# Splitting the last 512 tokens 384 + 128 instead of 256 + 256, and giving GpSimd two of the last eight multiplies

## The chip, the cores and the metric

The kernel runs on one core of a Trainium2 chip. The metric is the device time of one execution in microseconds (us). Three timed runs of the kernel before gave 1228.05, 1231.03 and 1229.72 us; their median is 1229.72 us.

The core has five engines that each work off their own queue in order: TensorE (PE in the profile; its weight loads are listed apart, as PEld), VectorE (DVE), ScalarE (ACT), GpSimd (POOL) and SyncE (SP), which here issues all DMA transfers. Engines wait for one another by semaphores. In this kernel TensorE writes its results to an accumulator memory, PSUM, from which VectorE and ScalarE read; everything else on the chip is held in the main memory of the engines, SBUF.

## What is computed

Two residual layers over 1024 tokens with 1024 features, each with a mixer (`h = RMSNorm(x) * (1 + scale(c)) + shift(c)`, then `x <- x + gate(c) * mixer(h)`), and a last RMSNorm. The change touches only the end: the output projection of the second mixer, its residual, and the last norm.

```python
    out = rms_norm(out, ...)                 # inside the mixers
    return (out * jax.nn.silu(g)) @ w_out    # odd mixer: the projection of the last stage
    ...
    x = x + gate[:, None, :] * y
return rms_norm(x, final_g)                  # x * rsqrt(mean(x*x) + eps) * final_g
```

## The kernel before

All data are held with the features on the 128 partitions and the tokens along the columns, so x is eight tiles ("slabs") of 128 features, each in two halves of 512 tokens (`HF`). A matrix product in float32 accuracy is made of three products of split operands (`mm3`, lines 196 to 199): high by high, high by low and low by high part. Each of the three loads a weight tile of 128 x 128 and then streams the tokens of the segment as its columns.

The last stage is lines 1259 to 1277, with `out_layer` (lines 939 to 1006). It goes through the tokens in three segments, `(0, 0, 0, 512)`, `(0, 1, 0, 256)` and `(0, 1, 256, 512)`: the first half of the tokens whole, then the second half in two pieces of 256. For every segment, `run` makes eight output slabs. One slab c is

- 8 x 3 products into one PSUM bank (`proj`, line 226; lines 197 to 199 in the profile, tile `pp`). There are four banks in turn;
- `evac`, line 960: VectorE adds the gated product to the residual x, in place (line 962, tile `xh`); ScalarE squares it (line 967, tile `sq`); VectorE adds the square to the sum of those before (line 973). In the last segment the square of the last slab isn't added but goes to TensorE by itself (lines 969 to 971), to spare a step at the end.

When a segment's eight slabs are done, `tail` (line 982) finishes the norm: TensorE sums the squares over the partitions with a tile of ones (`ss_add`, line 323, tile `ssl`), ScalarE takes the root (line 346, `rs`), VectorE the reciprocal (line 347, `rr`), TensorE spreads it over all partitions (`spread`, line 352, tile `bc`, in PSUM), and `finish` (line 1261) multiplies each slab by the norm's gain g and by `bc` (VectorE, line 1263) and stores it (SyncE, line 1265). Matrix products in full float32, such as those of lines 323 and 352, are two passes each in the profile: four calls are x8.

The loop at the end sets the order: with each slab of a segment, two steps of the tail of the segment before are issued (`some(before, 2)`), so the tails of the first two segments lie beside the products of the next. The tail of the last segment has nothing beside it. SyncE's queue takes the eight stores of a tail in the order of the slabs, 0 to 7. All weights of this stage are in SBUF, split into their two parts, by the end of its first segment: GpSimd's last work before the change (line 182) is there.

Of the kernel before, what the change touches and what calls it, by code (L numbers as in the profile page):

```python
# [11 lines left out]
F32 = mybir.dt.float32  # L12
F32R = mybir.dt.float32r
I32 = mybir.dt.int32
AF = mybir.ActivationFunctionType
ALU = mybir.AluOpType
# [3 lines left out]
P = 128  # L20
# [3 lines left out]
HF = 512  # L24
EPS = 1e-6
NEG = -1.0e38
LR = 12
SQ = 4
NM = (2, 2, 2)
NW = (3, 3, 3, 3)  # L30
# [18 lines left out]
O_FG = 72  # L49
# [47 lines left out]
def kernel(ctx, tc, xT, xTp, small, lamp, adaw, tb, w0, gw, wo0, w1, nab, wo1, out):  # L97
    nc = tc.nc
    V, A, G, T = nc.vector, nc.scalar, nc.gpsimd, nc.tensor
# [16 lines left out]
    sm = const.tile([P, N_SMALL], F32, tag="sm", name="sm")  # L116
# [93 lines left out]
    def wide(on):  # L210
        state["wide"] = on
# [3 lines left out]
    def split_act(k, hf, src, eng):  # L215
        hi = actp.tile([P, HF], F32R, tag=f"hi{k}_{hf}", name=f"ahi{k}_{hf}")
        lo = actp.tile([P, HF], F32R, tag=f"lo{k}_{hf}", name=f"alo{k}_{hf}")
        A.activation(hi[:], src, AF.Copy)
        eng.tensor_tensor(lo[:], src, hi[:], ALU.subtract)
        hact[k, hf] = (hi, lo)  # L220
# [5 lines left out]
    def proj(i, hf, evac, korder=range(KC), prep=True, view=lambda x: x, cols=(0, HF)):  # L226
        ks = list(korder)
        wh, wl = slab(i)
        ps = bank(f"pp{i}_{hf}")[:, :cols[1] - cols[0]]
        for n, k in enumerate(ks):  # L230
            hi, lo = (t[:, cols[0]:cols[1]] for t in hact[k, hf])
            mm3(ps, wh[:, k, :], wl[:, k, :], view(hi), view(lo), n == 0, n == KC - 1)
            if n % 2 == 1 and n < KC - 1:
                yield 1300.0
        with tc.high_priority():
            evac(hf, ps)
        if prep:
            ahead(i + 1)
        yield 1300.0
# [78 lines left out]
    def ss_start(name):  # L318
        return ptp.tile([P, HF], F32, tag="pt", name=name)

    def ss_add(ss, sq, start, stop, w=P):
        for j in range(4):
            T.matmul(ss[32 * j:32 * j + 32, :w], ones[:], sq[:, j * w:(j + 1) * w],
                     start=start, stop=stop)

    def rstd_rows(ss, n, pool, spare=None, add=EPS):


        if spare is not None:
            v, rr, t = (spare[:, i * P:(i + 1) * P] for i in range(3))  # L330
        else:
            v, rr, t = (pool.tile([P, P], F32, tag=g, name=g)[:] for g in ("rs", "rr", "rt"))
        V.tensor_scalar(v, ss[:, :P], 1.0 / n, add, ALU.mult, ALU.add)
        V.tensor_scalar(rr.bitcast(I32), v.bitcast(I32), -0.5, float(0x5F3759DF),
                        ALU.mult, ALU.add)
        for _ in range(3):
            V.scalar_tensor_tensor(t, rr, -0.5, rr, ALU.mult, ALU.mult)
            V.tensor_tensor(t, t, v, ALU.mult)
            V.scalar_tensor_tensor(rr, t, 1.5, rr, ALU.add, ALU.mult)
        return rr  # L340

    def rstd_rows_act(ss, n, pool, w):

        v = pool.tile([P, P], F32, tag="rs", name="rs")
        rr = pool.tile([P, P], F32, tag="rr", name="rr")
        A.activation(v[:, :w], ss[:, :w], AF.Sqrt, bias=eps[:], scale=1.0 / n)
        V.reciprocal(rr[:, :w], v[:, :w])
        return rr

    def spread(rr, bc, w=P):  # L350
        for j in range(4):
            T.matmul(bc[:, j * w:(j + 1) * w], sel[:, j, :], rr[:, :w], start=True, stop=True)
# [105 lines left out]
    with tc.tile_pool(name="start", bufs=2) as stp, tc.tile_pool(name="ada0", bufs=12) as adp:  # L458
# [11 lines left out]
        def squares(hf, on_dve, pool, tag):  # L470
# [4 lines left out]
            for k in range(KC):  # L475
                sq = stp.tile([P, HF], F32, tag="sq", name="sq", bufs=SQ)
                if k in on_dve:
# [5 lines left out]
        bcs = {}  # L483
# [131 lines left out]
    def some(gen, n):  # L615
        for _ in range(n):
            next(gen, None)
# [8 lines left out]
    with tc.tile_pool(name="lru", bufs=1) as lp:  # L626
# [34 lines left out]
        def pair(cs_):  # L661
# [3 lines left out]
            for c in cs_:  # L665
                xc, xh, xl = xcs[c]
                wh, wl = gws.pop(c)
                for r in range(2):
                    for g in range(2):
                        t = lp.tile([P, S], F32, tag="lr", name=f"t{g}", bufs=LR)  # L670
                        tt[c, r, g] = t
                        i = r * 2 + g
                        o = O_GB + (r * 2 + g) * 4 + c
                        for hf in range(2):
# [4 lines left out]
                            yield 648.0  # L679
                    w = ws[c, r] = lp.tile([P, S], F32, tag="lr", name="w", bufs=LR)  # L680
                    o = r * 4 + c
# [257 lines left out]
    def out_layer(l, ato, xsrc, xdst, pool, korder, view, segments):  # L939

        xs, acc, sums = {}, {}, {}

        def run(s):
            i0, hf, lo, hi = segments[s]
            n, w = hi - lo, (hi - lo) // 4

            def load(k):
                if k < KC and (k, hf) not in xs:  # L950
                    t = pool.tile([P, HF], F32, tag="xh", name=f"xh{l}_{hf}_{k}",
                                  bufs=11 if l == 0 else 16)
                    nc.sync.dma_start(t[:], xsrc[k * P:(k + 1) * P, hf * HF:(hf + 1) * HF])
                    xs[k, hf] = t

            load(0)
            for c in range(KC):
                load(c + 1)

                def evac(hf_, ps, c=c):  # L960
                    x = xs[c, hf][:, lo:hi]
                    state["dve"] = V.scalar_tensor_tensor(  # L962
                        x, ps, modc[l][:, 16 + c:17 + c], x, ALU.mult, ALU.add).ins
                    if xdst is not None:
                        nc.sync.dma_start(xdst[c * P:(c + 1) * P, hf * HF:(hf + 1) * HF], x)
                    sq = pool.tile([P, HF], F32, tag="sq", name="sq", bufs=3)
                    A.activation(sq[:, :n], x, AF.Square)
                    last = l and s == len(segments) - 1
                    if c == KC - 1 and last:
                        ss_add(sums[s], sq, False, True, w)  # L970
                        return
                    if c:
                        V.tensor_tensor(sq[:, :n], sq[:, :n], acc[s][:, :n], ALU.add)
                    acc[s] = sq
                    if c == KC - 2 and last:
                        sums[s] = ss_start(f"ssl{l}_{s}")
                        ss_add(sums[s], sq, True, False, w)
                for _ in proj(ato + i0 + c, hf, evac, korder, view=view, cols=(lo, hi)):
                    pass
                yield  # L980

        def tail(s, final):
            _, hf, lo, hi = segments[s]
            w = (hi - lo) // 4
            if s not in sums:
                sums[s] = ss_start(f"ssl{l}_{s}")
                with tc.issue_after(state["pe"]):
                    ss_add(sums[s], acc[s], True, True, w)
            if xdst is None:
                rr = rstd_rows_act(sums[s], D, pool, w)  # L990
            else:
                rr = rstd_rows(sums[s], D, pool)
                yield
            bc = ptp.tile([P, HF], F32, tag="pt", name=f"bc{l}_{s}")
            with tc.issue_after(state["pe"]):
                spread(rr, bc, w)
            yield
            for k in range(KC):
                final(k, hf, lo, xs[k, hf][:, lo:hi], bc[:, :hi - lo])
                yield  # L1000

        for hf in range(2):
            for k in korder:
                split_act(k, hf, mixed[k][:, hf * HF:(hf + 1) * HF],
                          G if l == 0 and k >= 4 else V)
        return run, tail
# [251 lines left out]

    wide(True)
    with tc.tile_pool(name="fin", bufs=2) as fp:  # L1260
        def finish(k, hf, lo, x, bc):
            g = sm[:, O_FG + k:O_FG + k + 1]
            V.scalar_tensor_tensor(x, x, g, bc, ALU.mult, ALU.mult)
            t0 = hf * HF + lo
            nc.sync.dma_start(out[k * P:(k + 1) * P, t0:t0 + x.shape[1]], x)


        segments = ((0, 0, 0, 512), (0, 1, 0, 256), (0, 1, 256, 512))
        run, tail = out_layer(1, ato1, x1d, None, fp, KORDER1, lambda x: x, segments)
        before = iter(())  # L1270
        for s in range(len(segments)):
            r = run(s)
            for c in range(KC):
                some(r, 1)
                some(before, 2)
            before = tail(s, finish)
        some(before, KC + 1)
# [100 lines left out]
```

## Time and profile before

| | |
|---|---|
| timed runs | 1228.05, 1229.72, 1231.03 us |
| profiled execution | 1229.11 us, its span 1227.2 us |
| PE, PEld busy in the span | 1177.9 us (96%), 969.2 us (79%) |
| DVE, ACT, POOL busy | 725.6 us (59%), 553.5 us (45%), 376.3 us (31%) |
| granted TensorE clock | 0.995 |

Times in the views are us from the start of the span; means of groups are in ns. `out<-in` names the tiles that an instruction writes and reads, and `128x256` is partitions by columns. A chain of waits follows the work that ended last back from step to step; "issue" in it is time in which the profile shows no wait. The ends of matrix products and weight loads are modelled by the profiler, so their starts say more than their durations.

### The profile page before, as it was taken

Reading aid. Unit: us, or ns where it says so; the run is one execution under the profiler, and the core shown is the slowest. Engines: PE = TensorE matmul, PEld = TensorE weight load, DVE = VectorE, ACT = ScalarE, POOL = GpSimd, SP = SyncE. Lnnn points to the kernel's source line nnn. Section 1 sums busy time; section 2 is a strip of 40 time slices with the busy share of each in tenths; the row PEclk is TensorE's granted clock in tenths of the full one; section 3 lists DMA queues with packets and bytes.
Section 4 is the critical chain, followed back from the end, with each engine's and each line's share of the span. In section 5 each row is a group of like instructions: output and inputs, shape, how many; then the busy total and the mean of one; then the engine's idle time right before and its main releaser. Section 6 shows DMA issues by size and latency. Waiting matters only on the chain.

```text
span 1227.2 us, 19073 instructions
## 1 busy us (share of the span) xinstructions
PE 1177.9 (96%) x7232; PEld 969.2 (79%) x7232; DVE 725.6 (59%) x1418; ACT 553.5 (45%) x1023; POOL 376.3 (31%) x348
## 2 busy tenths in 40 slices
PE   4989999799999999999999999999999999999997
PEld 3578887678888888777778888888988898877896
DVE  6762966899899889668672433453333323464344
ACT  3337658456666556423342333443344324375121
POOL 2113432133243334533422323333323333244100
PEclk9999999999999999999999999999999999999999
DMA  9610153232123110286424443333332333223312
GB/s 330 188 38 27 60 170 105 69 101 78 42 63 108 46 57 20 84 284 205 149 72 149 124 145 109 117 116 108 100 108 81 103 105 106 76 81 113 136 69 70
DMA packets 81467, 132.24 MB, mean 108 GB/s; under 512 B 7008, under 2 KB 48096, under 8 KB 81376
## 3 DMA queue, kind: packets, MB, share of 16 engines
q1 hardware_dynamic: 81376, 131.03, 34.1%
q8 instruction: 57, 0.93, 0.3%
q14 instruction: 34, 0.28, 0.1%
HBM read 110.03 MB, written 14.68 MB: 102 GB/s over the span
## 4 chain that ended last, share of the span: by engine, by line
PE 82%; DVE 10%; DMA 3%; ACT 2%; POOL 1%; issue 1%; SPq 0%; DVEq 0%; ACTq 0%; POOLq 0%
PE pp L197 16%; PE pp L199 16%; PE pp L198 15%; PE no L1226 4%; PE etr L1202 3%; PE v L197 3%; PE v L198 2%; PE v L199 2%; PE atr L857 2%; PE s L599 2%; PE s L600 2%; PE n L599 2%; PE n L600 2%; PE o L198 1%; PE o L197 1%
## 5 line engine op out<-in xcount | busy, mean ns | idle before, releaser
L197 PE MATMUL pp<-ahi,whi 128*128 128x512 f32 (+1 forms) x1040 | 405.9, 390 | 3.7 <-DVE sgb L605 3.3
L199 PE MATMUL pp<-ahi,wlo 128*128 128x512 f32 (+1 forms) x1040 | 397.4, 382 | 2.5 <-POOL wlo L182 2.5
L198 PE MATMUL pp<-alo,whi 128*128 128x512 f32 (+1 forms) x1040 | 395.8, 381 | 0.0
L182 POOL TENSOR_TENSOR wlo<-raw,whi 128x1024 fp32r<-128x1024 f32 x80 | 196.1, 2454 | 333.5 <-ACT whi L181 330.0
L197 PEld LDWEIGHTS pp<-ahi,whi 128*128 128x128 f32 x1040 | 196.3, 189 | 45.8 <-issue 9.6
L199 PEld LDWEIGHTS pp<-ahi,wlo 128*128 128x128 f32 x1040 | 196.3, 189 | 41.1 <-POOL wlo L182 3.4
L198 PEld LDWEIGHTS pp<-alo,whi 128*128 128x128 f32 x1040 | 196.5, 189 | 32.2 <-issue 0.7
L1182 DVE CUSTOM_DVE_ANT_0 e<-n,bias 128x288 f32<-128x288 f32 (+1 forms) x128 | 60.4, 504 | 151.8 <-PE n L600 76.7
L181 ACT ACTIVATE whi<-raw 128x1024 fp32r<-128x1024 f32 x80 | 84.3, 1055 | 133.4 <-PE pp L198 88.2
L1190 POOL TENSOR_SCALAR e<-e,r 128x288 f32<-128x288 f32 (+1 forms) x128 | 72.3, 577 | 180.0 <-DVE r L1188 178.0
L1185 ACT ACTIVATE e<-e,nm 128x288 f32<-128x288 f32 (+1 forms) x128 | 72.8, 570 | 111.9 <-DVE nm L1182 111.2
L831 ACT ACTIVATE e<-e,nm 128x1024 f32<-128x1024 f32 x64 | 73.4, 1148 | 38.3 <-DVE nm L827 37.7
L827 DVE CUSTOM_DVE_ANT_0 e<-s,tb 128x1024 f32<-128x1024 f32 x64 | 76.9, 1216 | 3.9 <-DMA tb<-in_tb_dram 2.6
L197 PE MATMUL v<-whi,ahi 128*128 128x256 f32 x256 | 74.7, 292 | 0.0
L198 PE MATMUL v<-wlo,ahi 128*128 128x256 f32 x256 | 72.5, 283 | 0.0
L199 PE MATMUL v<-whi,alo 128*128 128x256 f32 x256 | 72.3, 282 | 0.0
L848 POOL TENSOR_SCALAR e<-e,r 128x256 f32<-128x256 f32 x32 | 32.9, 1028 | 100.6 <-DVE r L837 42.4
L1226 PE MATMUL no<-et,vc 96*64 96x128 f32 (+1 forms) x768 | 60.6, 282 | 0.0
L1226 PEld LDWEIGHTS no<-et,vc 96*64 96x64 f32 (+1 forms) x768 | 42.2, 136 | 21.5 <-issue 19.3
L864 ACT ACTIVATE ath<-atr 128x512 fp32r<-128x512 f32 x64 | 38.0, 596 | 45.7 <-PE atr L857 45.4
L1206 ACT ACTIVATE et<-etr 96x384 f32<-96x384 f32 (+1 forms) x64 | 31.2, 487 | 58.8 <-DVE et L1208 53.7
L962 DVE SCALAR_TENSOR_TENSOR xh<-pp,mod,xh 128x512 f32<-128x512 f32 (+1 forms) x40 | 25.7, 643 | 53.8 <-PE pp L199 47.7
(206 smaller groups left out, 2007.6 us busy)
## 6 DMA issues: line engine op xcount, KB each, us to landing
raw<-in_w_dram SPq DMA_DIRECT2D x56, 512.0 KB
ada<-in_adaw_dram SPq DMA_DIRECT2D x96, 256.0 KB
raw<-in_wo_dram SPq DMA_DIRECT2D x24, 512.0 KB
bias<-in_nab_dram SPq DMA_DIRECT2D x32, 288.0 KB
qq<-qq SPq DMA_DIRECT2D x48, 128.0 KB
bias<-in_nab_dram SPq DMA_DIRECT2D x16, 384.0 KB
xT<-in_xT_dram SPq DMA_DIRECT2D x16, 256.0 KB
xh<-in_xTp_dram SPq DMA_DIRECT2D x16, 256.0 KB
```

The costliest lines, as they stand in the source:

```text
L181: A.activation(hi[:], raw[:], AF.Copy)
L182: G.tensor_tensor(lo[:], raw[:], hi[:], ALU.subtract)
L197: T.matmul(ps, lh, rh, start=start, stop=False)
L198: T.matmul(ps, lh, rl, start=False, stop=False)
L199: state["pe"] = T.matmul(ps, ll, rh, start=False, stop=stop).ins
L599: T.matmul(dst, qsel(q[m]), k, start=True, stop=False)
L827: state["dve"] = V.tensor_tensor_reduce(out=e[:], in0=ps[:].rearrange("p a b -> p (a b)"), in1=tbt[h][:, o:o + S], scale=-1.0, scalar=3.0e ...
L831: A.activation(e[:], e[:], AF.Exp, scale=-1.0, bias=nm[:], accum_out=sums[:, m:m + 1])
L1182: state["dve"] = V.tensor_tensor_reduce(out=e[:, m, :n], in0=ps[:, m, :n], in1=bias["now"][:, m, :n], scale=-1.0, scalar=3.0e38, op0=ALU.a ...
L1185: A.activation(e[:, m, :n], e[:, m, :n], AF.Exp, scale=-1.0, bias=nm[:, m:m + 1], accum_out=sums[:, m:m + 1])
L1190: state["pool"] = G.tensor_scalar(e[:, m, :n], e[:, m, :n], r[:, m:m + 1], 0.0, ALU.mult, ALU.add).ins
L1226: T.matmul(po[64 * m:64 * m + 64, b * P:(b + 1) * P], vch[p, b][:kn, j + hf, 64 * m:64 * m + 64], et[:kn, m, j * P:(j + 1) * P], start=(j ...
```

## The change

Two edits in the last stage.

First, the border between the last two segments moves from token 256 of the second half to token 384 (`LAST`): the middle segment has 384 tokens, the last 128.

Second, in the last segment slabs 0 and 1 (`EARLY`) are finished in another way. Right after their square is taken, ScalarE multiplies them by the gain g, in place. When `bc` is there, ScalarE copies it to an SBUF tile (`bcs`), and GpSimd multiplies the two slabs by that tile. The other six are multiplied by VectorE as before. The stores stay on SyncE, in the order 0 to 7.

```diff
+LAST = 384
+EARLY = (0, 1)
...
                     A.activation(sq[:, :n], x, AF.Square)
                     last = l and s == len(segments) - 1
+                    if last and c in EARLY:
+                        A.activation(x, x, AF.Copy, scale=sm[:, O_FG + c:O_FG + c + 1])
...
+        spread_ = {}
+
         def finish(k, hf, lo, x, bc):
             g = sm[:, O_FG + k:O_FG + k + 1]
-            V.scalar_tensor_tensor(x, x, g, bc, ALU.mult, ALU.mult)
+            if lo == LAST and k in EARLY:
+
+                if not spread_:
+                    spread_[0] = fp.tile([P, P], F32, tag="bcs", name="bcs", bufs=1)
+                    A.activation(spread_[0][:], bc, AF.Copy)
+                G.tensor_tensor(x, x, spread_[0][:], ALU.mult)
+            else:
+                V.scalar_tensor_tensor(x, x, g, bc, ALU.mult, ALU.mult)
...
-        segments = ((0, 0, 0, 512), (0, 1, 0, 256), (0, 1, 256, 512))
+        segments = ((0, 0, 0, HF), (0, 1, 0, LAST), (0, 1, LAST, HF))
```

## The prediction, made before the changed kernel was run

> **What bounds the kernel now.** I read the page first, for the span:
>
> ```profile
> span 1227.2 us, 19073 instructions
> ```
>
> The profiled execution took 1229.11 us, 1.91 us more than its span and 0.61 us less than the median of the three runs, 1229.72 us. The change touches only the last stage, so the next view is the busy time by stretches, for one inside the 512-token segment and one inside the last segment (256 tokens).
>
> ```profile
> 1145.00:1168.00 23.00, 23.00 (x105) 19.11 (x105) 6.94 (x10) 2.53 (x4) 0.32 (x1) 1.00 0.06 23
> 1198.00:1215.00 17.00, 17.00 (x144) 17.00 (x142) 7.94 (x19) 2.50 (x6) 0.00 (x0) 1.00 0.19 63
> ```
>
> The columns are the stretch's length, then PE, PEld, DVE, ACT and POOL busy, then the granted clock. TensorE (PE) has no idle time in either, so up to the last product the stage is bound by TensorE. The second number is the weight loads (PEld): 19.11 of 23.00 us with 512 columns to a product, but 17.00 of 17.00 with 256. With half the columns, a load is in flight at every moment.
>
> Then the chain that ended last, after TensorE's last product:
>
> ```profile
> 1217.03 0.49 DVE xh L962
> 1217.53 0.02 issue
> 1217.55 0.42 ACT sq L967
> 1217.97 0.04 issue
> 1218.02 0.36 PE ssl L323 x8
> 1218.38 0.02 issue
> 1218.40 0.32 ACT rs L346
> 1218.73 0.02 issue
> 1218.75 0.56 DVE rr L347
> 1219.31 0.14 issue
> 1219.45 1.09 PE bc L352 x8
> 1220.54 0.02 issue
> 1220.56 0.48 DVE xh L1263
> 1221.04 0.39 DVEq L1372
> 1221.44 2.35 DVE xh L1263 x6
> ```
>
> Here each step waits for the one before. From 1217.03 to the end of the span are 10.2 us, and only this tail can become shorter by a smaller last segment. Its last part isn't VectorE's but SyncE's:
>
> ```profile
> 1221.07 3.76 SPq L1265 DMA_DIRECT2D out_dram<-xh  x8
> ```
> ```profile
> L1265 SPq DMA_DIRECT2D out_dram<-xh x24: 332/361/403, 1175.7 to 1224.4; - x24
> ```
>
> VectorE is done at 1223.79 (1221.44 + 2.35), and SyncE's eighth issue ends at 1224.83. The second row gives the shortest, median and longest issue in ns. With 0.36 us for the last one, the starts are (3.76 − 0.36)/7 = 0.486 us apart, slower than the multiplies (2.35/6 = 0.39). The span ends 2.37 us after the last issue.
>
> **The change, part 1: what TensorE pays.** Each output slab has 8 × 3 = 24 products in every segment, whatever its number of tokens. The pitch of slabs is seen in the starts of VectorE's evacuations. With 512 columns, then with 256:
>
> ```profile
> 1151.38 0.75 DVE L962 SCALAR_TENSOR_TENSOR xh<-pp,mod,xh 128x512 f32<-128x512 f32 x1 [3.24 <-PE pp L199]
> 1152.83 0.69 DVE L973 TENSOR_TENSOR sq<-sq 128x512 f32<-128x512 f32 x1 [0.70 <-ACT sq L967]
> 1156.82 0.75 DVE L962 SCALAR_TENSOR_TENSOR xh<-pp,mod,xh 128x512 f32<-128x512 f32 x1 [3.30 <-PE pp L199]
> ```
> ```profile
> 1207.96 0.48 DVE L962 SCALAR_TENSOR_TENSOR xh<-pp,mod,xh 128x256 f32<-128x256 f32 x1 [1.42 <-PE pp L199]
> 1208.93 0.43 DVE L973 TENSOR_TENSOR sq<-sq 128x256 f32<-128x256 f32 x1 [0.48 <-ACT sq L967]
> 1210.84 0.48 DVE L962 SCALAR_TENSOR_TENSOR xh<-pp,mod,xh 128x256 f32<-128x256 f32 x1 [1.49 <-PE pp L199]
> ```
>
> 1156.82 − 1151.38 = 5.44 us per slab, 0.2267 per product; 1210.84 − 1207.96 = 2.88, 0.120 per product. So 256 columns cost 0.1067 us and each product 0.0133 besides. On that line 384 columns cost 4.16 us a slab (0.173 a product) and 128 cost 1.60 us (0.067). If the line held to the end, moving 128 tokens from one segment to the other would cost TensorE nothing: 4.16 + 1.60 = 2 × 2.88.
>
> I don't think that it holds below 256, because every product loads a weight tile of 128 columns, and the loads are already back to back. What such a load costs when little streams behind it is shown by the broadcast of line 352: eight passes, each with a 128-column weight load and only 64 columns.
>
> ```profile
> 1219.42 0.97 PEld L352 LDWEIGHTS bc<-rr,sel 128*128 128x128 f32 x8 [1.25 <-issue]
> ```
>
> The groups by form (the number after the bar's comma is the mean in ns) have the duration of one such load, and the pieces that the rest of the sum needs:
>
> ```profile
> L962 DVE SCALAR_TENSOR_TENSOR xh<-pp,mod,xh 128x256 f32<-128x256 f32 x16 | 7.7, 484 | 18.3 <-PE pp L199 18.3
> ...
> L1263 DVE SCALAR_TENSOR_TENSOR xh<-xh,sm,bc 128x512 f32<-128x512 f32 x8 | 5.7, 740 | 0.4 <-PE bc L352 0.4
> ...
> L352 PEld LDWEIGHTS bc<-rr,sel 128*128 128x128 f32 x24 | 2.9, 191 | 1.3 <-issue 1.2
> ...
> L962 DVE SCALAR_TENSOR_TENSOR xh<-pp,mod,xh 128x512 f32<-128x512 f32 x2 | 1.5, 752 | 6.6 <-PE pp L199 6.6
> ...
> L967 ACT ACTIVATE sq<-xh 128x512 f32<-128x512 f32 x2 | 1.3, 632 | 9.6 <-DVE xh L962 9.6
> ...
> L323 PE MATMUL ssl<-sq,ones 128*32 128x64 f32 x24 | 1.0, 231 | 1.0 <-ACT sq L967 1.0
> L347 DVE RECIPROCAL rr<-rs 128x128 f32<-128x128 f32 x1 | 1.0, 952 | 0.3 <-ACT rs L346 0.3
> ...
> L323 PE MATMUL ssl<-sq,ones 128*32 128x128 f32 x8 | 0.4, 285 | 0.0
> ```
>
> With 0.19 us for the last of the eight loads, their starts are (0.97 − 0.19)/7 = 0.111 us apart. How long 64 columns stream in these full-precision passes is seen in line 323: 64 more of them cost 285 − 231 = 54 ns. By the slab pitch 128 columns of this stage's products cost 0.1067/2 = 53 ns. So a pass of line 352 is the very case that the change makes: 54 ns of streaming behind a 128-column load. It starts every 0.111 us, not every 0.067. The last segment's slab then costs 24 × 0.111 = 2.66 us, not 1.60. The bounds are 1.60 (the line) and 2.88 (no gain at all over 256 columns); I take the row that has the same load and the same streaming time.
>
> The Trainium skill ("TensorE: Matmul & The Clock Gate", section LDWEIGHTS) gives a load's time as its columns over 1.2 GHz, whatever streams: an estimate of 107 ns here. By it the slab would cost 2.56 us and the sum below be 0.8 us lower; the row's 0.111 stays, since it has the gaps in it.
>
> For 384 columns there is one more row, the logits of line 599, in the chain:
>
> ```profile
> 917.02 0.18 PE n L599
> ```
>
> That is 0.18 a product against 0.173 by the line. Those products read their columns in rows of a grid, so I keep the line, and 0.18 as the upper bound: 192 × 0.007 = 1.3 us more.
>
> Sum for TensorE: eight slabs of the middle segment, 8 × (4.16 − 2.88) = +10.24 us; eight of the last, 8 × (2.66 − 2.88) = −1.76 us. Net **+8.5 us**, all on the path, as PE had no idle time to give.
>
> **Part 2: the tail with 128 tokens.** Evacuation 0.49 by 128/256 × (752 − 484) = 0.13 less; square 0.42, by half of (0.63 − 0.42), 0.11 less; the reciprocal goes from 64 to 32 columns and loses half of (0.95 − 0.56), 0.20. The sums, the root and the broadcast lose a few hundredths each, 0.09 together at a guess, for the broadcast's eight loads stay: its 1.09 us are load-bound as shown. Together −0.53 us.
>
> Then the store. Now the first multiply takes 0.48 and SyncE issues at 1221.07, 0.53 us after the broadcast. After the change slab 0 waits for ScalarE's copy of the broadcast and GpSimd's multiply:
>
> ```profile
> L306 ACT ACTIVATE macc<-mrow 128x128 f32<-128x128 f32 x8 | 2.2, 274 | 5.3 <-PE mrow L323 5.3
> ```
> ```profile
> L849 POOL TENSOR_TENSOR e<-e,e 128x256 f32<-128x256 f32 x32 | 24.2, 756 | 2.6
> ...
> L219 POOL TENSOR_TENSOR alo<-y,ahi 128x512 fp32r<-128x512 f32 x8 | 10.8, 1364 | 3.7 <-ACT ahi L218 3.5
> ```
>
> The copy is 0.27 us. GpSimd's multiply is 0.756 at 256 and 1.364 at 512 columns, hence 0.45 at 128. With three hand-overs of 0.02 the first store is issued 0.78 us after the broadcast, 0.25 later than now. Queued behind that wait on SyncE are the other seven stores, and their order is fixed. GpSimd's second result comes 0.45 later, in time for the second issue (0.486). VectorE's six multiplies (about 0.35 each by the evacuation's slope), even if they waited for the copy, would be ahead of SyncE. So the two slabs taken off VectorE bring nothing here, as VectorE wasn't what SyncE waited for at the end, and their detour costs +0.25. Bytes halve: an issue or landing may be quicker by 0 to 0.24 us each way, since 128 KB were absorbed every 0.486; I take −0.12 for the landing and nothing for the pitch. If the pitch fell to the bare 0.36, 7 × 0.126 = 0.9 us more would go.
>
> ScalarE's two scalings of slabs 0 and 1 and VectorE's eight multiplies of the middle segment (between 0.48 and 0.74 each) lie under 21 us of products; VectorE was busy 7.94 of 17 us. Without that cover they would cost about 6 us. Nothing waits for GpSimd then: it is idle in this stage.
>
> Tail: −0.53 + 0.25 − 0.12 = **−0.4 us**, between −1.5 and +0.3.
>
> Sum: +8.5 − 0.4 = +8.1 us, span 1235.3, against the median 1229.72 + 8.1 = **1237.8 us**, 0.7% slower. From no change a measurement here can tell about 0.2%, 2.5 us.
>
> **The rivals.** (a) The loads hide completely: TensorE keeps to the line, 1.60 us a slab, and the split is free. Then only the tail counts: 1229.3 us, no slower. For it: loads overlap with products everywhere in this stage. Against it: line 352's pitch of 0.111. It decides if the last segment's slab takes under 1.65 us.
>
> (b) Loads overlap one another in part: their durations (0.19) already overlap at starts 0.111 apart. At a pitch half way between 0.067 and 0.111, 0.089, a slab costs 2.14 us, TensorE +10.24 − 5.92 = +4.3, and the time is 1233.6. The same page of the Trainium skill (section Back-to-back issue gap) has a sustained figure of about 81 ns for pairs of load and product with 128 columns; by that estimate it would be 1232.1 us. Nothing here shows such a pitch with 128-column loads.
>
> (c) The load isn't hidden at all behind so short a product: 0.111 + 0.053 = 0.164, 3.94 us a slab, 1248.0 us. Against it: in line 352 54 ns of streaming fit inside 0.111.
>
> **How the numbers follow.** The forecast 0.84, (a) 0.06, (b) 0.07, (c) 0.03. The forecast's own bounds: 1236.7 with the shortest tail; 1237.8 + 1.7 (0.120 a product) + 1.3 (0.18) + 0.7 = 1241.5. The runs of before spread by 1.5 us to a side, which carries the low end to 1235; I take it to 1234 for part of (b). Range 1234 to 1242; outside are (a), most of (b), (c) and some 0.05 of the forecast. Faster by over 0.2% needs (a) and over 2 us more from the tail: 0.03. Same is the rest of (a) and the fast end of (b): 0.06. Slower: 0.91.
>
> **What would show it.** In the profile after, the evacuations of line 962 should start 4.16 us apart in the 384-token segment and 2.66 apart in the last; PEld should be busy throughout, and the last product should come about 8.5 us later than 1217.0. The first store of the tail should be issued 0.78 us after the broadcast, not 0.53, and the eight stores stay about 0.49 apart. A last slab pitch near 1.6 us would make the prediction wrong in its main step; a tail shorter by over 1.5 us would show the store queue misjudged.

## The result, and the profile after

The changed kernel took 1241.41 us (median of six runs, 1238.45 to 1242.55), the kernel before 1227.89 us in six runs beside them (1227.14 to 1231.03). The ratio is 1.0099, with a 95% interval of 1.0085 to 1.0112: slower by some 12.2 us, between 10.4 and 13.8 (the two medians lie 13.5 apart). The forecast was +8.1 us. The profiled execution took 1241.48 us, and its span is 12.5 us longer than that of before:

```profile
span 1239.7 us, 19077 instructions
```

I cut the span at two points that both kernels have: the start of the last evacuation of 512 columns (1167.70 before, 1168.82 after), and the start of the last evacuation of all. Up to the first, both give TensorE the same work in the same order, and the +1.1 us there is no effect of the change: the same cut lies anywhere from 1164.9 to 1170.8 in the profiles below that have the same work ahead of it. What follows is "the stage" between the two points, and "the tail" behind the second.

The stage, by VectorE's timeline; the evacuations are on line 964 now (962 before), and the products' lines are 199 to 201:

```profile
1199.45 0.62 DVE L964 SCALAR_TENSOR_TENSOR xh<-pp,mod,xh 128x384 f32<-128x384 f32 x1 [2.39 <-PE pp L201]
1203.61 0.62 DVE L964 SCALAR_TENSOR_TENSOR xh<-pp,mod,xh 128x384 f32<-128x384 f32 x1 [2.39 <-PE pp L201]
...
1221.69 0.35 DVE L964 SCALAR_TENSOR_TENSOR xh<-pp,mod,xh 128x128 f32<-128x128 f32 x1 [1.66 <-PE pp L201]
1224.37 0.35 DVE L964 SCALAR_TENSOR_TENSOR xh<-pp,mod,xh 128x128 f32<-128x128 f32 x1 [1.66 <-PE pp L201]
1228.64 0.35 DVE L964 SCALAR_TENSOR_TENSOR xh<-pp,mod,xh 128x128 f32<-128x128 f32 x1 [3.25 <-PE pp L201]
```

The 384-column slabs are 4.16 us apart and the 128-column slabs 2.68, or 0.112 per product. But the last slab comes 4.27 us after the one before it. Two things lie in there. First, a wait, by TensorE's timeline:

```profile
1224.62 0.27 PE L200 MATMUL pp<-alo,whi 128*128 128x128 f32 x1
1225.45 0.27 PE L325 MATMUL ssl<-sq,ones 128*32 128x32 f32 x8 [0.55 <-DVE sq L977]
```

The sums over the first seven squares stand in TensorE's queue among the products of the eighth slab. VectorE is done with the seventh square at 1225.40, and all products behind the sums wait until then. From 1224.62 to 1225.45 are 0.83 us; in the kernel before the same sums had no wait (the row has no bracket) and stood 0.21 us behind the product ahead of them:

```profile
1215.17 0.32 PE L323 MATMUL ssl<-sq,ones 128*32 128x64 f32 x8
```

There, 13 products of 0.120 us stood between the end of the seventh slab and the sums, 1.56 us for the three steps from evacuation to sum on VectorE and ScalarE, which took 1.39 (1213.72 to 1215.11); in the changed kernel 5 products of 0.112 stand there, 0.56 us for three steps of 1.03 (1224.37 to 1225.40). So it is their number, 5 instead of 13, that took the cover away, and hardly their pitch: 13 products of 0.112 would be 1.46 us. Second, the granted clock, in the windows of one us (the number behind POOL):

```profile
1226.00:1227.00 1.00, 1.00 (x11) 1.00 (x11) 0.00 (x0) 0.00 (x0) 0.00 (x0) 1.00 0.00 0
1227.00:1228.00 1.00, 1.00 (x8) 1.00 (x7) 0.00 (x0) 0.00 (x0) 0.00 (x0) 0.58 0.00 0
1228.00:1229.00 1.00, 0.60 (x3) 0.41 (x2) 0.35 (x1) 0.00 (x0) 0.00 (x0) 0.50 0.00 0
```

It falls to half about 1227.1, while TensorE is busy in 1.00 of 1.00 us, 1.5 us ahead of the last evacuation. In the kernel before it fell 5.2 us behind it, when TensorE was done for good:

```profile
1222.00:1223.00 1.00, 0.00 (x0) 0.00 (x0) 1.00 (x4) 0.00 (x0) 0.00 (x0) 0.62 0.81 265
```

The chain that ended last shows both the half-speed products and the tail (start, duration, what):

```profile
1225.10 0.30 DVE sq L977
1225.40 0.04 issue
1225.45 0.27 PE ssl L325 x8
...
1227.20 0.12 PE pp L201
1227.32 0.21 PE pp L199
1227.54 0.21 PE pp L200
...
1228.64 0.36 DVE xh L964
1229.00 0.02 issue
1229.03 0.32 ACT sq L969
1229.34 0.04 issue
1229.39 0.38 PE ssl L325 x8
1229.77 0.02 issue
1229.79 0.29 ACT rs L348
1230.09 0.02 issue
1230.11 0.36 DVE rr L349
1230.47 0.14 issue
1230.61 1.90 PE bc L354 x8
1232.51 0.02 issue
1232.53 0.28 ACT bcs L1273
```

Six products are 0.21 us apart instead of 0.11, and the broadcast, which TensorE also works off at half clock, takes 1.90 us instead of 1.09. One wait more lies ahead of all this, among the first products of the last segment: the broadcast of the middle segment's norm waits for VectorE's reciprocal. By TensorE's timeline it has 6 products between its sums and itself, where the kernel before has 9 and no wait (the changed kernel first):

```profile
1207.85 1.10 PE L354 MATMUL bc<-rr,sel 128*128 128x96 f32 x8 [0.53 <-DVE rr L349]
```
```profile
1196.36 1.08 PE L352 MATMUL bc<-rr,sel 128*128 128x64 f32 x8
```

Then the stores, of SyncE's timeline:

```profile
1233.42 3.65 SPq L1278 DMA_DIRECT2D out_dram<-xh  x8
```

The first is issued 0.91 us after the broadcast's end at 1232.51 (0.53 before). The last issue ends at 1237.07, and the span 2.63 us later (2.37 before), although each store has half the bytes.

The parts, in us (before, then after): up to the cut 1167.70 and 1168.82; the middle segment 24.46 and 34.79 (+10.33); the last 24.87 and 25.03 (+0.16); the tail 10.17 and 11.06 (+0.89).

### The profile page after: what moved, and what is told of

Read it like the earlier page. It is cut to its first block, busy times and chain, and to the rows that moved or that the text cites. A ratio compares the mean times of both kernels' runs of the same rounds, so it can differ in the third digit from the quotient of the medians.

```text
span 1239.7 us, 19077 instructions
## 1 busy us (share of the span) xinstructions
PE 1192.1 (96%) x7232; PEld 981.4 (79%) x7232; DVE 726.4 (59%) x1416; ACT 554.4 (45%) x1026; POOL 376.4 (30%) x350
## 4 chain that ended last, share of the span: by engine, by line
PE 82%; DVE 9%; DMA 3%; ACT 3%; issue 2%; POOL 1%; SPq 0%; DVEq 0%; ACTq 0%; POOLq 0%
PE pp L199 17%; PE pp L201 16%; PE pp L200 16%; PE no L1230 4%; PE etr L1206 3%; PE v L199 3%; PE v L200 2%; PE v L201 2%; PE atr L859 2%; PE n L601 2%; PE s L601 2%; PE n L602 2%; PE s L602 2%; DVE e L829 1%; PE o L200 1%
## 5 line engine op out<-in xcount | busy, mean ns | idle before, releaser
L199 PE MATMUL pp<-ahi,whi 128*128 128x512 f32 (+2 forms) x1040 | 410.8, 395 | 3.7 <-DVE sgb L607 3.3
L201 PE MATMUL pp<-ahi,wlo 128*128 128x512 f32 (+2 forms) x1040 | 402.0, 387 | 1.0 <-POOL wlo L184 1.0
L200 PE MATMUL pp<-alo,whi 128*128 128x512 f32 (+2 forms) x1040 | 400.3, 385 | 0.0
L964 DVE SCALAR_TENSOR_TENSOR xh<-pp,mod,xh 128x512 f32<-128x512 f32 (+2 forms) x40 | 25.7, 642 | 59.3 <-PE pp L201 54.4
```

The source lines that it names most:

```text
L199: T.matmul(ps, lh, rh, start=start, stop=False)
L200: T.matmul(ps, lh, rl, start=False, stop=False)
L201: state["pe"] = T.matmul(ps, ll, rh, start=False, stop=stop).ins
```

## The experiments

For every profile here: the stage and the tail as above, the broadcast's duration in the last tail, and when the granted clock fell, counted from the start of the last evacuation. In "whole" all evacuations have 512 columns, and its stage is counted from the eighth, which is the same point as in the others.

| kernel | span | stage | tail | broadcast | clock fell |
|---|---|---|---|---|---|
| before | 1227.2 | 49.33 | 10.17 | 1.09 | +5.2 |
| after | 1239.7 | 59.82 | 11.06 | 1.90 | −1.5 |
| after_2 | 1238.4 | 60.47 | 11.11 | 1.90 | −2.8 |
| after_3 | 1235.7 | 59.19 | 11.11 | 1.90 | 0.0 |
| split_only | 1235.6 | 59.20 | 10.18 | 1.90 | −0.1 |
| gpsimd_only | 1227.8 | 49.33 | 11.98 | 1.54 | +2.9 |
| narrow_first | 1240.3 | 58.10 | 11.36 | 1.12 | +4.8 |
| split_320 | 1230.2 | 54.51 | 9.67 | 1.08 | +4.0 |
| late_sums | 1237.3 | 58.23 | 10.18 | 1.06 | +3.6 |
| late_sums_2 | 1235.0 | 58.24 | 10.21 | 1.06 | +3.8 |
| late_sums_3 | 1236.7 | 58.23 | 10.19 | 1.06 | +3.7 |
| half_loads | 1226.7 | 50.47 | 11.01 | 1.90 | +1.7 |
| two_queues | 1225.3 | 48.90 | 9.52 | 1.10 | +3.4 |
| whole | 1225.2 | 45.69 | 14.65 | 2.06 | +3.5 |

**Each edit by itself.** The split alone, and the GpSimd part alone (with the border at 256):

```diff
-EARLY = (0, 1)
+EARLY = ()
```

> The border at token 384, but all eight last multiplies on VectorE as before (no scaling by ScalarE, no copy, no GpSimd). If the weight loads make the slower time (a product with a 128-column load starts no sooner than 0.111 us after the one before), the last segment's slabs stay 2.68 us apart and the middle ones 4.16, and the time stays at about 12 us above the kernel before; the first store of the tail comes about 0.37 us after the broadcast instead of 0.91, so 0.5 us at most is won back. If GpSimd's detour is a large part of what the prediction missed, 3 us or more are won back. The halving of TensorE's clock near the end should still be there, as nothing on TensorE changes.

```diff
-LAST = 384
+LAST = 256
...
-                    spread_[0] = fp.tile([P, P], F32, tag="bcs", name="bcs", bufs=1)
+                    spread_[0] = fp.tile([P, 256], F32, tag="bcs", name="bcs", bufs=1)
```

> The segments 256 and 256 as before, but slabs 0 and 1 of the last one scaled by ScalarE and multiplied by GpSimd (256 columns). Loads theory: TensorE as in the kernel before, slabs 2.88 us apart, clock at full speed to the last product; the first store comes 0.37 (copy) + 0.76 (GpSimd at 256 columns) + 0.07 after the broadcast, 1.2 us instead of 0.53, and the other seven follow 0.49 apart, so +0.7 us: within what a measurement can tell from no change. GpSimd theory: 3 us or more slower.

The split alone has the ratio 1.0084 (1.0067 to 1.0101), the GpSimd part alone 1.0005 (0.9996 to 1.0015). So the split is the loss; the GpSimd part can't be told from no change by time. Its price is seen in the traces. Split alone, by the chain and by SyncE's timeline:

```profile
1227.39 1.90 PE bc L354 x8
```
```profile
1229.69 3.65 SPq L1278 DMA_DIRECT2D out_dram<-xh  x8
```

The first store is issued 0.40 us after the broadcast (1229.29), not 0.91, and the span ends 2.26 us after the last issue, not 2.63. So the tail is 0.88 us shorter without the detour: 0.51 ahead of the first store, which is the detour's, and 0.37 behind the last issue, for which no run shows the reason. At 256 columns, the GpSimd part alone:

```profile
1218.24 1.54 PE bc L354 x8
```
```profile
1221.08 3.96 SPq L1278 DMA_DIRECT2D out_dram<-xh  x8
```

Here the first store comes 1.30 us after the broadcast (1219.78) instead of 0.53, the issues take 0.20 longer and the end 0.39; 0.45 us are the broadcast, into which the falling clock reached. That makes the tail 1.81 us longer at an unchanged stage. As nothing ahead of the broadcast takes another time than in the kernel before, where the clock fell 2.3 us later, the 0.45 aren't shown to be the edit's.

**The same narrow segment in another place.** The split turned round, 128 then 384, with all multiplies on VectorE:

```diff
-LAST = 384
-EARLY = (0, 1)
+LAST = 128
+EARLY = ()
```

> The second half of the tokens as 128 first and 384 last, all multiplies on VectorE. Loads theory: TensorE pays the same, 8 x 4.16 + 8 x 2.68 against 16 x 2.88, +8.6 us, wherever the narrow segment stands; the tail has 384 columns and is about 0.8 us longer than with 256 (evacuation +0.14, square +0.11, reciprocal +0.2, first store +0.13, multiplies 0.52 apart for stores 0.49 apart +0.2); the waits of TensorE in the last slab and the halved clock before the last product go, as 4.16 us of products cover them. So about +9 to +10 us. If the slower time belonged to a narrow LAST segment (waits, clock), it would be within 2 us of the kernel before.

Ratio 1.0078 (1.0058 to 1.0098). The stage is 8.77 us longer than before, the tail 1.19. By VectorE's timeline the narrow slabs cost the same in the middle:

```profile
1188.36 0.35 DVE L964 SCALAR_TENSOR_TENSOR xh<-pp,mod,xh 128x128 f32<-128x128 f32 x1 [1.66 <-PE pp L201]
1191.04 0.35 DVE L964 SCALAR_TENSOR_TENSOR xh<-pp,mod,xh 128x128 f32<-128x128 f32 x1 [1.66 <-PE pp L201]
```

2.68 us apart. The cost is the narrow segment's own, wherever it stands; what the change adds to it at the end, the early fall of the clock, is gone here (the clock fell 4.8 us behind the last evacuation).

**A width between.** The border at 320, with all multiplies on VectorE, so 320 and 192 columns:

```diff
-LAST = 384
-EARLY = (0, 1)
+LAST = 320
+EARLY = ()
```

> The second half as 320 and 192, all multiplies on VectorE. Loads theory: 192 columns cost as much as 128, 0.112 a product, 2.68 us a slab, and 320 cost 0.147, 3.52 us; 8 x (3.52 + 2.68 - 5.76) = +3.5 us on TensorE, and with the tail about -0.3 and up to 1.5 us of waits in the last segment +3 to +5. If the cost per column is a straight line (0.093 a product, 2.24 us a slab), TensorE pays nothing and the time is within 1.5 us of the kernel before.

Ratio 1.0030 (1.0019 to 1.0041). VectorE's timeline, first the wide slabs and then the narrow:

```profile
1188.59 0.55 DVE L964 SCALAR_TENSOR_TENSOR xh<-pp,mod,xh 128x320 f32<-128x320 f32 x1 [1.94 <-PE pp L201]
1192.10 0.55 DVE L964 SCALAR_TENSOR_TENSOR xh<-pp,mod,xh 128x320 f32<-128x320 f32 x1 [1.94 <-PE pp L201]
...
1211.17 0.42 DVE L964 SCALAR_TENSOR_TENSOR xh<-pp,mod,xh 128x192 f32<-128x192 f32 x1 [1.42 <-PE pp L201]
1213.85 0.42 DVE L964 SCALAR_TENSOR_TENSOR xh<-pp,mod,xh 128x192 f32<-128x192 f32 x1 [1.47 <-PE pp L201]
```

A slab of 192 columns costs 2.68 us, exactly as much as one of 128: at these widths there is a floor, not a slope, 0.20 us under a slab of 256. With 3.51 for 320 columns that is 8 × (3.51 + 2.68 − 2 × 2.88) = +3.4 us; the stage grew by 5.18, by 1.7 us more. Most of that lies in the same two waits as in the changed kernel, 0.61 us at the broadcast of the middle segment and 0.85 at the sums, which here have only 4 products ahead of them:

```profile
1217.79 0.29 PE L325 MATMUL ssl<-sq,ones 128*32 128x48 f32 x8 [0.85 <-DVE sq L977]
```

Yet the clock didn't fall early here, but 4.0 us behind the last evacuation.

**The load itself.** This is the direct test of whether the load sets the floor, or each product has one of its own. The products of the 128-token segment load only 64 of the 128 weight columns; their number and the 128 tokens that they stream stay:

```diff
+            if cols[1] - cols[0] == P:
+                mm3(ps[0:64], wh[:, k, 0:64], wl[:, k, 0:64], view(hi), view(lo),
+                    n == 0, n == KC - 1)
+            else:
+                mm3(ps, wh[:, k, :], wl[:, k, :], view(hi), view(lo), n == 0, n == KC - 1)
...
+                    r = P if n != P else 64
...
-                        x, ps, modc[l][:, 16 + c:17 + c], x, ALU.mult, ALU.add).ins
+                        x[:r], ps[:r], modc[l][:r, 16 + c:17 + c], x[:r], ALU.mult, ALU.add).ins
```

> The changed kernel, but in the last segment each product loads 64 weight columns instead of 128 and computes only the lower half of its slab's features; the residual update of the upper 64 features of every slab is left out for the last 128 tokens. Number of products, columns streamed and waits are the same. Loads theory: the pitch of a product falls from 0.112 to 0.067 us (what 128 columns cost by the straight line) or somewhat more, the slabs come about 1.6 us apart instead of 2.68, and 8 us or so are won. If the floor belongs to the product itself (its issue, its write to PSUM) and not to the load's size, the slabs stay 2.68 us apart.

Ratio to the kernel before 1.0022 (1.0008 to 1.0036), against 1.0099 with full loads. In its trace, TensorE's timeline inside the segment:

```profile
1205.93 0.22 PE L199 MATMUL pp<-ahi,whi 128*64 128x128 f32 x1
...
1206.11 0.22 PE L199 MATMUL pp<-ahi,whi 128*64 128x128 f32 x1
```

Line 199 has every third product, so three start in 0.18 us: 0.060 apart instead of 0.112. The groups by form show what else became shorter, the load (mean 135 ns instead of 192):

```profile
L199 PEld LDWEIGHTS pp<-ahi,whi 128*64 128x64 f32 x54 | 7.3, 135 | 0.0
```
```profile
L199 PEld LDWEIGHTS pp<-ahi,whi 128*128 128x128 f32 x45 | 8.6, 192 | 0.0
```

The first row is of this kernel, the second of the changed one. The stage is 9.35 us shorter than with full loads. Half the weight columns also write half the outputs; that this isn't the reason is seen at 192 columns, which write half as many outputs again as 128 at the same 0.112. So the 128-column load is what holds a product at 0.112 us, and a floor of the product itself isn't there above 0.060.

**The wait for the sums, and the clock.** The sums over the first seven squares are put behind the last product of the eighth slab:

```diff
                     if c == KC - 1 and last:
+                        sums[s] = ss_start(f"ssl{l}_{s}")
+                        with tc.issue_after(state["pe"]):
+                            ss_add(sums[s], acc[s], True, False, w)
                         ss_add(sums[s], sq, False, True, w)
                         return
...
-                    if c == KC - 2 and last:
-                        sums[s] = ss_start(f"ssl{l}_{s}")
-                        ss_add(sums[s], sq, True, False, w)
```

> The changed kernel, with one thing moved: in the last segment the sums of squares of the first seven slabs go to TensorE after the last product, not among the products of the last slab. TensorE then no longer waits in the last slab for the seventh square (0.7 us), and the eight short passes (0.3 us) lie under the last evacuation and square. If it was this gap that made the clock fall before the last product, it now falls only in the tail or after it: the last products keep 0.112 us (0.6 us won), the broadcast takes about 1.1 us instead of 1.90, and about 2.2 us are won in all. If products with 128 columns, streaming half the time, make the clock fall by themselves, it falls before the last product again and only about 1 us is won. The slabs stay 2.68 us apart in either case, so the time stays 9 to 11 us above the kernel before.

Ratio 1.0080 (1.0062 to 1.0097); by time alone it can't be told from the changed kernel's 1.0099 (1.0085 to 1.0112). The traces tell them apart. TensorE's timeline has no wait any more between the last product and the sums:

```profile
1226.81 0.28 PE L201 MATMUL pp<-ahi,wlo 128*128 128x128 f32 x1
1227.02 0.27 PE L325 MATMUL ssl<-sq,ones 128*32 128x32 f32 x8
```

The broadcast, in the chain, is back at full speed, and so is the clock in its window:

```profile
1229.03 1.06 PE bc L354 x8
```
```profile
1229.00:1230.00 1.00, 0.97 (x8) 0.97 (x8) 0.00 (x0) 0.00 (x0) 0.00 (x0) 1.00 0.00 0
```

Stage and tail together are 68.41 us, against 70.88 for the changed kernel. As one profile could have met the clock by chance, both kernels were profiled twice more, unchanged:

> The changed kernel once more, for a second profile. If the 0.7 us gap in the last slab is what lets the clock fall early, it falls again before or within 0.5 us of the last product, and the last broadcast takes about 1.9 us. If the early fall was an accident of where a window of the clock's control stood, it may now come 3 us or more after the last product, as it did where the sums were moved.

> The changed kernel with the sums moved behind the last product, for a second profile. If the gap is what lets the clock fall early, it falls again some 3 us or more after the last product and the broadcast takes about 1.1 us. If the first was an accident of a window's place, it can fall before or at the last product here too.

> A third profile of the changed kernel, with the same expectations as the second.

> A third profile of the changed kernel with the sums moved, with the same expectations as the second.

With the wait, among products of 128 columns with full loads (after, after_2, after_3, split_only), the clock fell at or ahead of the last evacuation in four profiles of four, and the broadcast took 1.90 us each time. Without it, it fell 3.6 to 3.8 us behind in three of three, and the broadcast took 1.06. Stage and tail together are 70.3 to 71.6 us in the changed kernel and 68.4 without the wait. So the wait and the clock together cost the change 1.9 to 3.2 us. The single times of these executions were 1240.1 and 1237.4 us (after_2, after_3), 1236.69 and 1238.45 (late_sums_2, late_sums_3), with 1230.79 for the kernel before beside them.

**Other ways to a shorter end.** In the kernel before, with the late sums of the diff above, the stores of the last tail are shared between two queues:

```diff
-            nc.sync.dma_start(out[k * P:(k + 1) * P, t0:t0 + x.shape[1]], x)
+            q = nc.scalar if lo == 256 and k % 2 else nc.sync
+            q.dma_start(out[k * P:(k + 1) * P, t0:t0 + x.shape[1]], x)
```

> The kernel before, with two edits that the findings point to: the sums of the first seven slabs after the last product, as above (TensorE loses the 0.4 us by which its last slab is longer), and in the last tail every second store issued by ScalarE's queue instead of SyncE's, so that the stores follow the multiplies (0.39 us apart) and not SyncE's issues (0.49 apart). If SyncE's issues bound the end, the tail is 0.6 us shorter, 1.0 us in all, which is less than a measurement can tell from no change; the trace would show it. If transfers and not issues bound it, only 0.4 us.

```profile
1219.83 2.68 SPq L1266 DMA_DIRECT2D out_dram<-xh  x4
1220.22 2.69 ACTq L1266 DMA_DIRECT2D out_dram<-xh  x4
```

By the two queues' timeline the eight issues now take 3.08 us (1219.83 to 1222.91) instead of 3.76. The stage is 0.43 us shorter and the tail 0.65, but the ratio is 0.9994 (0.9984 to 1.0004): a gain of that size is below what the times can tell. It is the best version that I found, and it isn't shown to beat the kernel before.

And the opposite of the change, no split at all:

```diff
-        segments = ((0, 0, 0, 512), (0, 1, 0, 256), (0, 1, 256, 512))
+        segments = ((0, 0, 0, 512), (0, 1, 0, 512))
```

> The kernel before without the split of the second half: one segment of 512 tokens. Straight-line part of the cost: 8 x 5.44 instead of 16 x 2.88, -2.6 us, and one set of sums and broadcast less among the products, -1.3 us. The tail with 512 columns: evacuation +0.27, square +0.21, sums and root +0.15, reciprocal +0.40, first multiply +0.27, then multiplies 0.68 apart instead of stores 0.49 apart +1.4, landing up to +0.3: +2.9 us. Together about -1 us, within what can be told from no change. If short tails were worth more than TensorE's per-product cost, it would be slower by 2 us or more.

```profile
1214.01 2.06 PE bc L352 x8
```
```profile
1216.87 4.94 SPq L1265 DMA_DIRECT2D out_dram<-xh  x8
```

By the chain and SyncE's timeline, the broadcast is at half clock here too and the issues take 4.94 us. TensorE gains 3.64 us of stage, and the tail of 512 columns gives back 4.48: ratio 1.0016 (1.0005 to 1.0026). The split 256 + 256 is worth having, by little.

## Why the prediction was right, and where it was short

The direction and the mechanism were right: the loads bound the narrow segment. The time lies inside the range, 1234 to 1242, but the size was 4 us short, and that 1241.41 is still inside is partly luck: the upper end was made of a pitch of 0.120 and of 0.18 per product, neither of which came, and what filled the room were waits, the fallen clock and, in the profiled execution, 1.1 us from ahead of the change. By the prediction's steps:

- **Middle segment, +10.24 us.** Measured +10.33, with slabs 4.16 us apart as forecast. The bound of 0.18 per product wasn't needed.
- **A slab of 128 columns, 2.66 us.** Measured 2.68. The weight load of the broadcast was the right row to take: products that stream the same 128 columns start every 0.112 us with the full load and every 0.060 with half of it. The Trainium skill ("TensorE: Matmul & The Clock Gate", section LDWEIGHTS) gives an estimate of 107 ns for the load, which agrees with the 112 ns measured to 5 ns.
- **The last segment, 8 × (2.66 − 2.88) = −1.76 us. This is the term that failed:** measured +0.16. The narrower products did save 8 × (2.88 − 2.68) = 1.60, and three things took it back. From the product ahead of the sums to the second behind them are 1.19 us instead of 0.68 (+0.5), the same stretch about the broadcast of the middle segment is 1.83 instead of 1.22 (+0.6), and six products at half clock cost about 0.6. The step "all on the path, as PE had no idle time to give" counted TensorE's products and not the short work queued between them. The number of products that stand ahead of that work isn't the same in the two kernels: 13 became 5 at the sums, 9 became 6 at the broadcast, whose reciprocal also grew with the middle segment, from 0.56 us to 0.75. What sets these numbers no run here shows.
- **The smaller steps of the tail, −0.53.** Evacuation 0.36, square 0.32, reciprocal 0.36 and root 0.29 came as worked out; with the sums at 0.38 that is −0.44. But the broadcast, said to keep its 1.09, took 1.90 at half clock: +0.81, the largest miss of the tail.
- **The detour by ScalarE and GpSimd, +0.25.** The copy (0.28 us) and GpSimd's multiply (0.43) were as estimated, but the first store came 0.91 us after the broadcast, not 0.78: GpSimd started 0.13 us after the copy's end (1232.94 after 1232.81), where 0.02 was allowed. That is +0.38 against the kernel before. Against the split alone the detour costs 0.51 there.
- **Landing, −0.12.** Measured +0.26. With all multiplies on VectorE it is −0.11 (2.26), so it isn't the bytes; why it is longer with the detour stays open (narrow_first, without the detour and with stores of 192 KB, has the same 2.63). The eight issues took 3.65 us instead of 3.76, so their pitch stayed, as forecast.
- **Tail together, −0.4.** Measured −0.44 + 0.81 + 0.38 − 0.11 + 0.26 = +0.90, by cut +0.89: outside the bounds given for it, −1.5 to +0.3.

The rest of the profiled 12.5 us is the +1.1 ahead of the change. Rivals (a) and (b), with 1.60 and 2.14 us a slab, and (c), with 3.94, all fell to the 2.68.

## What to carry to other kernels

A product costs at least the load of its weights, here 0.112 us for 128 columns; with 128 or 192 columns to stream it costs the same, so a segment cut below 256 tokens buys next to nothing on TensorE (2.68 us a slab instead of 2.88), and the tokens moved elsewhere are paid in full. When a segment is made smaller, look in the new trace at the short work that is queued between its products: count the products that stand ahead of it, for their number can change (5 instead of 13 here), and compare their time with that of the steps that make its inputs. And price a tail's matrix products at the clock that will be granted by then, not at that of the old trace.

## What the runs showed of the hardware that was not expected

- The granted clock fell to half while TensorE was working, 1.7 us after a wait of under 1 us (1225.45 to about 1227.1; 1.0 to 2.5 us in after_2, after_3 and split_only), in a stretch of products that by the slab pitch stream for 53 of their 112 ns. The Trainium skill ("TensorE: Matmul & The Clock Gate", section "HAM oscillation") has it that gaps of over some 3.4 us are to be avoided; no gap of that length is here. The wait of 0.53 us at the middle broadcast, in the same kind of products, brought no fall in any of these profiles, half_loads, whose products stream nearly without pause (53 of 60 ns), had waits of 0.87 and 0.84 us and kept the clock until 1.7 us behind the last evacuation, and split_320, with 192 columns (80 of 112 ns), waited 0.85 us at the sums and kept it until 4.0 us behind. So such a wait isn't enough by itself. What the control counts stays open; that the changed kernel's early fall needs the wait at the sums is shown by the runs with and without it.
- SyncE takes 3.65 us for eight stores of 64 KB and 3.76 for eight of 128 KB: at these sizes the pitch is hardly one of bytes. Shared between two queues, four stores took 2.68 us in each, as in each queue a store waits for every second of VectorE's multiplies, which are 0.39 us apart; what two queues could do without that no run shows.
- A load of 64 weight columns lets products start every 0.060 us, one of 128 every 0.112. As 53 of the 60 ns are streaming, the smaller load may be shorter still.
